# Gate and up blocks by Strassen's seven products for three of eight k-tile pairs, and the feed forward in parts of 4, 4 and 3 blocks

## The chip, the cores and the metric

The kernel runs on one core of one Trainium2 chip. The core has a matrix engine (PE, which reads its stationary operand through a weight load, PEld), a vector engine (DVE), a scalar engine (ACT), GpSimd (POOL) and a queue engine (SP) that issues DMAs. The metric is the device time of one execution in microseconds (us).

## What is computed

The input is 256 tokens of width 2048 in float32. The reference runs two blocks: a hybrid layer (an mLSTM and a gated delta net side by side), and a layer of dilated attention and gated linear attention followed by a feed forward. The change is in that feed forward, which is the last stage:

```
h = rmsnorm(x, ffn_norm_w[l])
x = x + (jax.nn.silu(h @ w_gate[l]) * (h @ w_up[l])) @ w_down[l]
```

`w_gate` and `w_up` are 2048 x 5632, `w_down` is 5632 x 2048, all float32. A final rmsnorm follows.

## The kernel before

**Every product is three matmuls.** A float32 matrix is split into a high part (`fp32r`, the rounded value) and a low part (the difference). A product is `hi x wh + hi x wl + lo x wh`. The activations' `hi` and `lo` (tiles `hl`, `pg`) are stationary operands of 128 x 128; the weights' `wh` and `wl` are the moving operands, 512 columns wide, and the sums stand in PSUM (tile `mm`), one bank for each half `t` of the 256 tokens.

**The weight stream.** All weights of the whole kernel pass through one list of pieces in a fixed order. A piece is up to three k-tiles (128 rows) of a 512-column block, at most 1536 columns wide (`WN`). For piece `i` the stream issues the load of piece `i + 3` on SP (tile `wr`, `RB` = 3 buffers), then the split of pieces up to `i + 2`, then the matmuls of piece `i`. The split (`cut`, L259 and L260) is a cast on ACT into `wh`, and then a subtraction on DVE into `wl`; `wh` and `wl` have three buffers each. So ACT can cast a piece only when PE has finished with the piece that held the buffer, three pieces earlier. What follows a finished chunk (its activation function, transposes, the operand for the next stage) runs as a generator in `sides`, one step for each piece or so.

**The feed forward.** It runs in two halves of 2816 hidden columns, each of five blocks of 512 columns and one of 256. For each block a gate chunk (16 k-tiles, two banks) is followed by `ff_gate` (tanh on ACT, two DVE operations), then an up chunk, then `ff_up`: multiply, transpose by PE (L203), cast on ACT (L1354) and subtraction on DVE (L1355) into the operand for the down projection. After each half come four down chunks of 22 k-tiles, each ended by `ff_down`, two DVE operations that add into the residual `hw`.

**The order of instructions.** A scheduler orders each engine's queue when the program is built; each engine then works its queue in order. [...]

Of the kernel before, what the change touches and what calls it, by code (L numbers as in the profile page):

```python
# [11 lines left out]
F32 = mybir.dt.float32  # L12
# [25 lines left out]
HALF = HID // 2  # L38


C_ID, C_TRIU, C_TRIL, C_MNEG, C_SEG, C_ONE, C_HB, C_VEC = 0, 128, 256, 384, 512, 768, 770, 818
# [56 lines left out]
        self.po = None  # L98


class Opnd:


    def __init__(self, n):
        self.t = [None] * n
        self.cols = [0] * n

    def ready(self, k):
        return self.cols[k] == 1
# [7 lines left out]

    def lo(self, k, t=None):
        return self.part(1, k, t)

@with_exitstack
def kernel(ctx, tc, a, out, dbg=None):
# [35 lines left out]
    def v3(t, b):  # L160
        return t.rearrange("p (a b) -> p a b", b=b)
# [72 lines left out]

# [2 lines left out]
    def load(i):  # L237
        if i >= len(pieces) or i in raw:
            return
        ch, k, n = pieces[i]  # L240
        w = wp.tile([P, WN], F32, tag="wr", name=nm("wr"), bufs=RB)
        wv = v3(w[:, :n * ch.width], ch.width)
        c = 0
        for src in ch.src:
            cw_ = src.shape[1]
            SP.dma_start(out=wv[:, :, c:c + cw_],  # L246
                         in_=src[(ch.k0 + k) * P:(ch.k0 + k + n) * P, :].rearrange("(k p) n -> p k n", p=P))
            c += cw_
# [29 lines left out]
    def products(ch, k0, tiles, ks, o):  # L278

        for j in ks:  # L280
# [10 lines left out]
            else:  # L291
# [3 lines left out]
                mm(po, wl, hi, start=False, stop=False)  # L295
                mm(po, wh, lo, start=False, stop=last)

    def run_stream():
        i = 0
        while i < len(pieces):  # L300
            ch, k0, _ = pieces[i]

            many = LAST if i == len(pieces) - LAST else 1
            for j in range(many):
                load(i + j + 3)
            for j in range(3):
                cut(i + j)
            tiles = []
# [62 lines left out]
    def vec(row):  # L371
        return vt[:, row:row + 1]
# [926 lines left out]
    sc3 = cst.tile([P, 2], F32, name="sc3")  # L1299
    st_3 = {"n": 0}  # L1300

    def mix_out(po, n):
        h = v3(hw[n], 512)
        for t in range(2):
# [9 lines left out]
        yield from operand(h, op3, 4 * n, 4, lambda j: vec(V_FN + 4 * n + j), act3["t"][0], act3["t"][1], 4 * n)  # L1314
        if n == 3:
            m_ = small(2, "ms2")
            V.tensor_reduce(out=m_, in_=v3(ss3, 4), axis=AX.X, op=ALU.add)
# [2 lines left out]
            ts(r3h, r3, 0.5)  # L1320
            stt(sc3, r3, 0.5, r3, ALU.mult, ALU.mult)

    opf = [Opnd(44), Opnd(44)]
    gate = {}

    def ff_gate(po, key, w):

        n = page()[:, :2 * w]
        n3 = v3(n, w)
        for t in range(2):  # L1330
            act(n3[:, t, :], po[t][:, :w], AF.Tanh, scale=r3h[:, t:t + 1])
# [32 lines left out]
    def ff_down(po, n, hf):  # L1364
# [4 lines left out]
        if hf == 1:  # L1369
# [111 lines left out]
    for hf in range(2):  # L1481
        off = 0
        while off < HALF:
            w = min(512, HALF - off)
            c0 = hf * HALF + off
            add(Chunk([wg[:, c0:c0 + w]], w, 16, op3, lambda po, c0=c0, w=w: ff_gate(po, c0, w)))
            add(Chunk([wu[:, c0:c0 + w]], w, 16, op3, lambda po, c0=c0, hf=hf, w=w: ff_up(po, c0, w, hf, c0 // P)))
            off += w
        for n in range(4):
            add(Chunk([wd[:, n * 512:(n + 1) * 512]], 512, HALF // P, opf[hf],  # L1490
                      lambda po, n=n, hf=hf: ff_down(po, n, hf), k0=hf * HALF // P))
# [25 lines left out]
```

## Time and profile before

| what | value |
|---|---|
| three runs | 2348.87, 2351.42, 2351.17 us; median 2351.17 |
| the profiled execution | 2350.77 us, of which the span from the first to the last instruction is 2349.0 us |
| busy share of the span | PE 99%, weight load 82%, DVE 59%, ACT 45%, POOL 4% |
| granted PE clock, mean | 0.998 of full speed |
| gate and up loads begin | 1600.0 us |
| last output DMA issued from | 2341.2 us |

Busy time is the time in which an engine had an instruction in work. A chain of waits names what the end of the program waited for, step by step backwards.

### The profile page before, as it was taken

The numbers are of one execution on the slowest core, as the hardware profiler recorded it, in microseconds if no ns is written. First come the engines' busy times: TensorE is split into PE (matmuls) and PEld (weight loads), VectorE is DVE, ScalarE is ACT, GpSimd is POOL, SyncE is SP. The second block draws the span as 40 slices with busy tenths as digits, with TensorE's granted clock in tenths as the row PEclk, the third lists the DMA queues.
The fourth block names the chain that finished last, engine by engine and source line by source line (L and its number), as shares of the span: only waits on it lengthen the run. The fifth ranks groups of instructions, "written<-read, shape, count | busy, mean of one in ns | idle before, by whom it ended". The sixth has DMA issues, their size and how long they took to land.

```text
span 2349.0 us, 28535 instructions
## 1 busy us (share of the span) xinstructions
PE 2330.5 (99%) x11392; PEld 1930.0 (82%) x11392; DVE 1384.8 (59%) x1689; ACT 1062.6 (45%) x1240; POOL 91.1 (4%) x122
## 2 busy tenths in 40 slices
PE   8999999999999999999999999999999999999998
PEld 6888888888888888888887877888888888888886
DVE  6778677686576555455555566655545544555554
ACT  5554444544454444444444465444444333434443
POOL 0101001000000000000000000000000000000000
PEclk9999999999999999999999999999999999999999
DMA  6656545665555556566565544556655555665554
GB/s 207 188 177 202 180 142 157 188 196 188 169 159 163 180 188 210 184 200 210 180 219 179 157 141 130 166 180 201 188 192 186 191 191 187 192 194 187 188 197 152
DMA packets 226340, 427.89 MB, mean 182 GB/s; under 512 B 17256, under 2 KB 25872, under 8 KB 226208
## 3 DMA queue, kind: packets, MB, share of 16 engines
q1 hardware_dynamic: 220288, 411.07, 54.7%
q0 software_dynamic: 5056, 13.70, 2.1%
q8 instruction: 89, 1.46, 0.2%
q10 hardware_dynamic: 864, 1.31, 0.2%
q14 instruction: 43, 0.35, 0.0%
HBM read 422.31 MB, written 3.73 MB: 181 GB/s over the span
## 4 chain that ended last, share of the span: by engine, by line
PE 98%; DMA 1%; ACT 0%; issue 0%; DVE 0%; SPq 0%; POOLq 0%; POOL 0%; ACTq 0%; DVEq 0%
PE mm L185 91%; PE sp L185 4%; PE sp L203 3%; PE sp L699 1%; PE sp L1129 0%; DMA wr<-in_w_in_dram 0%; DMA pg<-in_x_dram 0%; ACT pg L182 0%; DVE wl L260 0%; ACT wh L259 0%; ACT hl L182 0%; SPq L246 0%; DVE pg L179 0%; ACT hp L182 0%; POOLq L1513 0%
## 5 line engine op out<-in xcount | busy, mean ns | idle before, releaser
L185 PE MATMUL mm<-wh,hl 128*128 128x512 f32 (+1 forms) x4864 | 1500.1, 387 | 1.6 <-ACT wh L259 1.6
L260 DVE TENSOR_TENSOR wl<-wr,wh 128x1536 fp32r<-128x1536 f32 (+3 forms) x588 | 919.3, 1567 | 751.6 <-ACT wh L259 750.7
L259 ACT CAST wh<-wr 128x1536 fp32r<-128x1536 f32 (+3 forms) x588 | 780.4, 1328 | 994.7 <-PE mm L185 943.1
L185 PEld LDWEIGHTS mm<-wh,hl 128*128 128x128 f32 x4864 | 904.7, 188 | 183.2 <-issue 4.9
L185 PE MATMUL mm<-wl,hl 128*128 128x512 f32 (+1 forms) x2432 | 941.9, 387 | 1.3 <-DVE wl L260 1.3
L185 PEld LDWEIGHTS mm<-wl,hl 128*128 128x128 f32 x2432 | 458.0, 188 | 89.7 <-DVE wl L260 1.9
L185 PE MATMUL mm<-wh,pg 128*128 128x512 f32 x1472 | 456.0, 390 | 0.0
L185 PEld LDWEIGHTS mm<-wh,pg 128*128 128x128 f32 x1472 | 276.2, 188 | 57.0
L185 PE MATMUL mm<-wl,pg 128*128 128x512 f32 x736 | 287.4, 390 | 0.0
L185 PEld LDWEIGHTS mm<-wl,pg 128*128 128x128 f32 x736 | 138.2, 188 | 29.2 <-DVE wl L260 0.9
L203 PE MATMUL sp<-con,pg 128*128 128x128 f32 x555 | 88.3, 275 | 4.1 <-DMA pg<-in_consts_dram 4.0
L203 PEld LDWEIGHTS sp<-con,pg 128*128 128x128 f32 x555 | 68.9, 141 | 21.0 <-issue 6.0
L179 DVE SCALAR_TENSOR_TENSOR pg<-cv,vt,pg 128x255 f32<-128x255 f32 (+2 forms) x144 | 61.4, 478 | 7.6 <-ACT pg L182 7.5
L185 PE MATMUL sp<-pg,pg 128*128 128x128 f32 (+3 forms) x320 | 50.7, 316 | 0.0
L179 DVE SCALAR_TENSOR_TENSOR pg<-pg,mm 128x512 f32<-128x512 f32 (+1 forms) x60 | 39.9, 665 | 16.5 <-ACT pg L182 14.8
L185 PEld LDWEIGHTS sp<-pg,pg 128*128 128x128 f32 (+1 forms) x320 | 43.0, 190 | 6.1 <-issue 2.5
L182 ACT ACTIVATE pg<-mm,rh 128x512 f32<-128x512 f32 x40 | 27.2, 687 | 33.8 <-PE mm L185 33.8
L182 ACT ACTIVATE pg<-pg 128x512 f32<-128x512 f32 (+2 forms) x54 | 35.3, 676 | 12.1 <-DVE pg L792 4.9
L182 ACT ACTIVATE pg<-mm,rstd 128x512 f32<-128x512 f32 x36 | 24.4, 687 | 32.2 <-PE mm L185 32.2
L182 ACT ACTIVATE pg<-sp,vt 128x256 fp32r<-128x256 f32 (+1 forms) x48 | 21.5, 471 | 25.7 <-PE sp L203 14.4
L179 DVE SCALAR_TENSOR_TENSOR hl<-sp,vt,hl 128x256 fp32r<-128x256 f32 x48 | 21.7, 479 | 14.0 <-ACT hl L182 13.9
L182 ACT ACTIVATE hl<-sp,vt 128x256 fp32r<-128x256 f32 x48 | 21.2, 478 | 16.1 <-PE sp L203 10.9
(245 smaller groups left out, 871.2 us busy)
## 6 DMA issues: line engine op xcount, KB each, us to landing
wr<-in_w_in_dram SPq DMA_DIRECT2D x208, 768.0 KB, 4.5
wr<-in_w_in_dram SPq DMA_DIRECT2D x104, 512.0 KB, 4.6
wr<-in_w_out_dram SPq DMA_DIRECT2D x48, 768.0 KB, 4.5
wr<-in_w_down_dram SPq DMA_DIRECT2D x48, 768.0 KB, 4.4
wr<-in_w_gate_dram SPq DMA_DIRECT2D x42, 768.0 KB, 4.4
wr<-in_w_up_dram SPq DMA_DIRECT2D x42, 768.0 KB, 4.4
wr<-in_w_out_dram SPq DMA_DIRECT2D x24, 512.0 KB, 5.1
wr<-in_w_gate_dram SPq DMA_DIRECT2D x20, 512.0 KB, 4.8
```

The lines of the kernel that those rows point to most:

```text
L179: return V.scalar_tensor_tensor(out=o, in0=x, scalar=s, in1=y, op0=op0, op1=op1)
L182: return A.activation(out=o, in_=x, func=f, **kw)
L185: PE.matmul(o, l, r, start=start, stop=stop)
L203: PE.transpose(o, x, ident[:n, :n])
L259: A.copy(out=h[:, :sz], in_=w[:, :sz])
L260: V.tensor_tensor(out=l[:, :sz], in0=w[:, :sz], in1=h[:, :sz].bitcast(F32), op=ALU.subtract)
L699: PE.matmul(o, l, r_, start=True, stop=True, tile_position=(row, col))
```

## The change

**Seven products.** A pair of k-tiles, two halves of the tokens, and gate and up side by side make a 2 x 2 by 2 x 2 product of blocks of 128 x 128 by 128 x 512. Before, that is eight products (24 matmuls). For pairs 1, 3 and 5 of the eight pairs of a block (`SPAIRS`, counted there from 0) the new kernel forms Strassen's seven products (Winograd's form, 21 matmuls) in three pieces: A (three products: 9 matmuls, 1536 columns to split), B and C (two products: 6 matmuls and 1024 columns each). The extra operands are sums: of the activations, made once in `operand3`; of the weights, made on DVE for each piece A by three subtractions (`cut`). Of C nothing is loaded; it is a page that these subtractions fill. The other five pairs stay at eight products in two pieces, X (the gate's two k-tiles) and Y (the up's), 12 matmuls and 1024 columns each. Seven sums stand in seven banks; `ff_mid` and `ff_done` add them up on DVE.

**Parts.** There are eleven blocks of 512, in parts of 4, 4 and 3 (`PARTS`), each part followed by its four down chunks (16, 16 and 12 k-tiles). The raw buffers `wr` become four, and the scratch of the POOL-issued DMAs goes from 8192 to 2048 bytes.

```diff
-RB = 3
+RB = 4
+AHEAD = 3
+SPAIRS = (0, 2, 4)
+PARTS = ((0, 4), (4, 8), (8, 11))
...
+    PLAN = {"X": (("2", "a0"), ("4", "a1")), "Y": (("5", "a1"), ("3", "d")),
+            "A": (("1", "a0", 0), ("2", "a0", 1), ("3", "s4", 2)),
+            "B": (("5", "s1", 0), ("7", "s3", 1)),
+            "C": (("6", "s2", 0), ("4", "a1", 1))}
...
+        elif part in "XY":
+            get(w[:, :1024], ch.src[part], k, 2)
+        elif part == "A":
+            get(w[:, :1024], ch.src["X"], k, 2)
+            get(w[:, 1024:], ch.src["Y"], k + 1, 1)
+        elif part == "B":
+            get(w[:, :512], ch.src["Y"], k, 1)
...
+        if part == "A":
+
+            w2, w3 = raw[i + 1], page()
+            raw[i + 2] = w3
+            V.tensor_tensor(out=v3(w2[:, 512:], 512), in0=mid(w2[:, :512], 2), in1=v3(w, 512)[:, 0::2, :], op=ALU.subtract)
+            V.tensor_tensor(out=w3[:, :512], in0=w[:, 1024:], in1=w2[:, 512:1024], op=ALU.subtract)
+            V.tensor_tensor(out=w3[:, 512:1024], in0=w[:, 512:1024], in1=w3[:, :512], op=ALU.subtract)
+        x = w[:, 512:] if part == "B" else w[:, :{None: n * ch.width, "X": 1024, "Y": 1024, "A": 1536, "C": 1024}[part]]
...
+    def pair_products(ch, e, k0, part, wh, wl):
...
+            for q in js:
...
+                mm(po, hi, wh[:, q, :], start=first, stop=False)
+                mm(po, hi, wl[:, q, :], start=False, stop=False)
+                mm(po, lo, wh[:, q, :], start=False, stop=last)
...
+            ch.po = {b: pm.tile([P, 512], F32, tag="mm", name=nm("mm")) for b in "2453"}
+        if part == "A" and "1" not in ch.po:
+            for b in "176":
+                ch.po[b] = ps.tile([P, 512], F32, tag="sp", name=nm("mm"))
...
+    def ff_mid(po, st):
+
+        x, v = page(), page()
+        A.copy(out=x[:, :512], in_=po["1"])
+        V.tensor_tensor(out=x[:, 512:], in0=x[:, :512], in1=po["6"], op=ALU.add)
+        V.tensor_tensor(out=v[:, :512], in0=x[:, 512:], in1=po["7"], op=ALU.add)
...
+    def ff_done(po, st, part, k0):
...
+        V.tensor_tensor(out=g[:, lo_], in0=x[:, lo_], in1=po["2"], op=ALU.add)
+        V.tensor_tensor(out=g[:, hi_], in0=v[:, lo_], in1=po["4"], op=ALU.add)
+        V.tensor_tensor(out=v[:, hi_], in0=x[:, hi_], in1=po["5"], op=ALU.add)
+        V.tensor_tensor(out=v[:, lo_], in0=v[:, lo_], in1=po["5"], op=ALU.add)
+        V.tensor_tensor(out=v[:, hi_], in0=v[:, hi_], in1=po["3"], op=ALU.add)
+        for t, c in ((0, lo_), (1, hi_)):
+            act(x[:, c], g[:, c], AF.Tanh, scale=r3h[:, t:t + 1])
+        yield
+        stt(g, x, 1.0, g, ALU.add, ALU.mult)
+        mul(g[:, lo_], g[:, lo_], v[:, hi_])
+        mul(g[:, hi_], g[:, hi_], v[:, lo_])
...
-        while off < HALF:
-            w = min(512, HALF - off)
...
+    for part, (b0, b1) in enumerate(PARTS):
+        for blk in range(b0, b1):
...
-    nc = bacc.Bacc("TRN2", target_bir_lowering=False, num_devices=1, dynamic_dma_scratch_size=8192)
+    nc = bacc.Bacc("TRN2", target_bir_lowering=False, num_devices=1, dynamic_dma_scratch_size=2048)
```

In the queues below, line numbers of the new kernel differ: L217 is the matmul (before L185), L317 the cast and L319 the subtraction of a split (before L259, L260), L311 to L313 the three subtractions for a piece A, L1484 to L1488 the five sums of `ff_done`, L211 and L202 a helper for its products.

DVE's queue before, where an up chunk ends and the next gate chunk follows. `wl` is a split's output, L170 multiplies by the up sums, L1355 makes the down operand:

```order
L260 TENSOR_TENSOR wl2031_12757<-wr2026_12730,wh2030_12756 128x1536
L170 TENSOR_TENSOR pg2011_12639<-pg2011_12639,mm2015_12650 128x512
L170 TENSOR_TENSOR pg2011_12639<-pg2011_12639,mm2016_12651 128x512
L260 TENSOR_TENSOR wl2034_12783<-wr2029_12754,wh2033_12782 128x1536
L260 TENSOR_TENSOR wl2042_12810<-wr2032_12780,wh2041_12809 128x1024
L1355 TENSOR_TENSOR pg2038_12801<-sp2039_12802,pg2037_12800 128x512
L260 TENSOR_TENSOR wl2045_12836<-wr2040_12807,wh2044_12835 128x1536
```

The same queue of the new kernel between the second and the third block. The rows begin behind the split of the last piece Y (`wl2094`) and L312; `wl2098`, `wl2100`, `wl2104` and `wl2114` are the next block's A, B, C and first X:

```order
L313 TENSOR_TENSOR pg2096_12895<-wr2092_12874,pg2096_12895 128x512
L1484 TENSOR_TENSOR pg2101_12931<-pg2081_12815,mm2034_12600 128x512
L319 TENSOR_TENSOR wl2098_12901<-wr2092_12874,wh2097_12899 128x1536
L1485 TENSOR_TENSOR pg2101_12931<-pg2082_12816,mm2035_12601 128x512
L319 TENSOR_TENSOR wl2100_12917<-wr2095_12893,wh2099_12915 128x1024
L1486 TENSOR_TENSOR pg2082_12816<-pg2081_12815,mm2036_12602 128x512
L1487 TENSOR_TENSOR pg2082_12816<-pg2082_12816,mm2036_12602 128x512
L1488 TENSOR_TENSOR pg2082_12816<-pg2082_12816,mm2037_12603 128x512
L319 TENSOR_TENSOR wl2104_12943<-pg2096_12895,wh2103_12941 128x1024
L211 SCALAR_TENSOR_TENSOR pg2101_12931<-pg2081_12815,pg2101_12931 128x1024
L311 TENSOR_TENSOR wr2121_12998<-wr2121_12998,wr2118_12983 128x1024
L319 TENSOR_TENSOR wl2114_12968<-wr2102_12939,wh2113_12966 128x1024
```

Between two splits there stood at most two rows of 512 columns before; now the sums of the finished block, the subtractions for two pieces A and a product of 1024 columns stand between them.

PE's queue of the new kernel at the same place: the last matmuls of B, those of C and X that need `wh` alone, and the first that needs X's `wl2114`:

```order
L217 MATMUL mm2107_12947<-wl2100_12917,pg1888_11793 128x512
L217 MATMUL mm2107_12947<-wh2099_12915,pg1888_11793 128x512
L217 MATMUL mm2106_12946<-wh2103_12941,hl1878_11738 128x512
L217 MATMUL mm2105_12945<-wh2113_12966,hl1878_11738 128x512
L217 MATMUL mm2106_12946<-wl2104_12943,hl1878_11738 128x512
L217 MATMUL mm2106_12946<-wh2103_12941,hl1878_11738 128x512
L217 MATMUL mm2106_12946<-wh2113_12966,hl1878_11738 128x512
L217 MATMUL mm2107_12947<-wh2119_12986,hl1878_11738 128x512
L217 MATMUL mm2108_12948<-wh2119_12986,cv1897_11858 128x512
L217 MATMUL mm2105_12945<-wl2114_12968,hl1878_11738 128x512
```

The scheduler has brought seven matmuls of C, X and Y forward, ahead of the first that reads `wl2114`; before, a piece's matmuls stood in their own order with whole pieces of 12 or 18.

ACT's queue of the new kernel a little later, around the block's second triple (pair 3): the casts of Y, A, B, C and of the X and Y behind them; L1506 belongs to the finished block:

```order
L317 CAST wh2119_12986<-wr2112_12964 128x1024
L317 CAST wh2123_13004<-wr2118_12983 128x1536
L317 CAST wh2126_13025<-wr2121_12998 128x1024
L1506 CAST pg2115_12976<-sp2117_12978 128x512
L317 CAST wh2129_13045<-pg2122_13000 128x1024
L317 CAST wh2132_13060<-wr2128_13043 128x1024
L317 CAST wh2135_13073<-wr2131_13058 128x1024
```

The cast of C (`wh2129`) reads a page that DVE writes (L312, L313), so it waits for DVE, and the casts of X and Y stand behind it; before, every cast read a loaded tile.

## Rows read from the trace of the kernel before

**Rows 1.** The page: the span, the busy time of each engine, and the granted PE clock in 40 slices.

```profile
span 2349.0 us, 28535 instructions
PE 2330.5 (99%) x11392; PEld 1930.0 (82%) x11392; DVE 1384.8 (59%) x1689; ACT 1062.6 (45%) x1240; POOL 91.1 (4%) x122
PEclk9999999999999999999999999999999999999999
```

**Rows 2.** The page: the chain of waits that ended last, by engine.

```profile
PE 98%; DMA 1%; ACT 0%; issue 0%; DVE 0%; SPq 0%; POOLq 0%; POOL 0%; ACTq 0%; DVEq 0%
```

**Rows 3.** The chain of waits in order of time, inside the feed forward: start us, length us, what, how many. L185 is the matmul, L203 a transpose; the last row is of the block of 256 columns.

```profile
1661.83 39.27 PE mm L185 x173
...
1705.89 0.44 PE sp L203 x4
1706.32 5.72 PE mm L185 x25
...
1833.61 2.27 PE mm L185 x19
```

**Rows 4.** Busy time in three stretches: from the first gate load issued of one block of 512 columns to that of the next, the block of 256 columns, and a half's down chunks. Columns: length, then busy us and instructions of PE, PEld, DVE, ACT, POOL, then granted PE clock, DMA share, GB/s.

```profile
1635.39:1679.89 44.50, 44.50 (x202) 36.77 (x201) 22.79 (x18) 18.52 (x16) 0.00 (x0) 1.00 0.61 189
1813.39:1836.95 23.56, 23.56 (x134) 20.71 (x133) 11.73 (x9) 9.31 (x8) 0.00 (x0) 1.00 0.64 209
1836.95:1958.44 121.49, 121.49 (x606) 103.46 (x605) 58.76 (x44) 45.20 (x35) 0.00 (x0) 1.00 0.56 191
```

**Rows 5.** Groups of instructions by shape: line, engine, operation, out<-in, shape, count, busy us, mean ns of one, idle time before and what ended it. The first eight are from 1600 us on, the last three of the whole trace.

```profile
L260 DVE TENSOR_TENSOR wl<-wr,wh 128x1536 fp32r<-128x1536 f32 x132 | 232.0, 1758 | 272.1 <-ACT wh L259 272.1
L259 ACT CAST wh<-wr 128x1536 fp32r<-128x1536 f32 x132 | 195.5, 1481 | 282.4 <-PE mm L185 282.4
L260 DVE TENSOR_TENSOR wl<-wr,wh 128x1024 fp32r<-128x1024 f32 x56 | 68.6, 1225 | 45.3 <-ACT wh L259 45.3
L259 ACT CAST wh<-wr 128x1024 fp32r<-128x1024 f32 x56 | 59.0, 1054 | 81.6 <-PE mm L185 81.6
L1355 DVE TENSOR_TENSOR pg<-sp,pg 128x512 fp32r<-128x512 f32 x22 | 15.1, 688 | 10.1 <-ACT pg L1354 10.0
L182 ACT ACTIVATE pg<-mm,r3h 128x512 f32<-128x512 f32 x20 | 13.8, 691 | 19.0 <-PE mm L185 19.0
L170 DVE TENSOR_TENSOR pg<-pg,mm 128x512 f32<-128x512 f32 x20 | 13.7, 684 | 3.1 <-PE mm L185 3.1
L179 DVE SCALAR_TENSOR_TENSOR pg<-mm,sc,pg 128x512 f32<-128x512 f32 x16 | 12.0, 748 | 8.1 <-PE mm L185 7.1
...
L179 DVE SCALAR_TENSOR_TENSOR pg<-pg,pg 128x1024 f32<-128x1024 f32 x10 | 12.2, 1220 | 0.7 <-ACT pg L182 0.6
L170 DVE TENSOR_TENSOR pg<-pg,pg 128x1024 f32<-128x1024 f32 x4 | 4.9, 1224 | 0.1
L775 DVE TENSOR_TENSOR pg<-pg,hp 128x512 f32<-128x512 f32 x4 | 2.7, 684 | 0.0
```

**Rows 6.** The timeline of DVE and ACT: start us, length us, engine, line, what, idle time before and what ended it. First ACT in an earlier stage, then both engines in the feed forward.

```profile
942.65 0.69 ACT L182 ACTIVATE pg<-mm,rh 128x512 f32<-128x512 f32 x1 [1.12 <-PE mm L185]
943.23 1.47 ACT L259 CAST wh<-wr 128x1536 fp32r<-128x1536 f32 x1
...
1694.03 1.76 DVE L260 TENSOR_TENSOR wl<-wr,wh 128x1536 fp32r<-128x1536 f32 x1 [3.28 <-ACT wh L259]
1695.70 0.68 DVE L170 TENSOR_TENSOR pg<-pg,mm 128x512 f32<-128x512 f32 x1
...
1699.31 1.06 ACT L259 CAST wh<-wr 128x1024 fp32r<-128x1024 f32 x1 [1.24 <-PE mm L185]
1700.40 1.23 DVE L260 TENSOR_TENSOR wl<-wr,wh 128x1024 fp32r<-128x1024 f32 x1 [0.53 <-ACT wh L259]
```

**Rows 7.** Who waited for whom from 1600 us on: total us, times, longest us.

```profile
ACT wh L259 <- PE mm L185: 374.5, 178, 3.0
DVE wl L260 <- ACT wh L259: 328.6, 183, 3.3
```

**Rows 8.** DMA issues: count, KB each, median us from issue to landing. The first two are from 1640 to 1812 us (gate and up), the third from 1840 to 1950 us (down).

```profile
wr<-in_w_gate_dram SPq DMA_DIRECT2D x16, 768.0 KB, 4.4
...
wr<-in_w_gate_dram SPq DMA_DIRECT2D x7, 512.0 KB, 5.3
...
wr<-in_w_down_dram SPq DMA_DIRECT2D x7, 512.0 KB, 3.7
```

**Rows 9.** Stretches with waits of PE, as in rows 4: two of the start, and the end.

```profile
8.00:12.00 4.00, 2.89 (x19) 2.34 (x17) 1.36 (x3) 3.72 (x12) 0.00 (x0) 1.00 0.96 295
...
24.00:28.00 4.00, 2.58 (x11) 1.47 (x9) 1.50 (x1) 3.00 (x6) 0.00 (x0) 1.00 0.70 258
...
2311.00:2349.00 38.00, 28.74 (x127) 23.47 (x125) 15.39 (x17) 12.57 (x18) 1.12 (x2) 0.93 0.35 126
```

**Rows 10.** Who waited in the whole trace: PE for split weights, and two of the waits for DMAs that POOL issues; the engine that waits comes first.

```profile
PE mm L185 <- ACT wh L259: 1.6, 2, 0.9
PE mm L185 <- DVE wl L260: 1.5, 3, 1.1
...
POOL hp L690 <- DMA xo<-pg: 6.1, 2, 3.1
POOL pg L583 <- DMA li<-pg: 5.3, 2, 3.4
```

More of the change, by code (lines that the diff above doesn't have):

```diff
@@ L98, in __init__ @@
         self.po = None
+class Pair:
+    kind, width = "pair", 512
+    PLAN = {"X": (("2", "a0"), ("4", "a1")), "Y": (("5", "a1"), ("3", "d")),
+            "A": (("1", "a0", 0), ("2", "a0", 1), ("3", "s4", 2)),
+            "B": (("5", "s1", 0), ("7", "s3", 1)),
+            "C": (("6", "s2", 0), ("4", "a1", 1))}
+    def __init__(self, x, y, nk, opnd, pairs, mid, done):
+        self.src, self.nk, self.opnd, self.mid, self.done, self.k0 = {"X": x, "Y": y}, nk, opnd, mid, done, 0
+        self.parts = []
+        for p in range(nk // 2):
+            self.parts += [(2 * p, 2, c) for c in ("ABC" if p in pairs else "XY")]
+        self.last_s = max(i for i, q in enumerate(self.parts) if q[2] == "C")
+        self.po = None
+        use = [(i, t[0]) for i, q in enumerate(self.parts) for t in self.PLAN[q[2]]]
+        self.first = {b: min(i for i, c in use if c == b) for _, b in use}
+        self.final = {b: max(i for i, c in use if c == b) for _, b in use}
 class Opnd:
@@ L224, in add @@
         chunks.append(ch)
+        if ch.kind == "pair":
+            pieces.extend((ch, k, n, c) for k, n, c in ch.parts)
+            return ci
         m = -(-ch.nk // ch.per)
@@ L239, in load, with get @@
             return
-        ch, k, n = pieces[i]
+        ch, k, n, part = pieces[i]
+        if part == "C":
+            raw[i] = None
+            return
         w = wp.tile([P, WN], F32, tag="wr", name=nm("wr"), bufs=RB)
[L242 to L248, printed above, removed]
-        raw[i] = w
+        raw[i] = w
+        def get(o, src, k, n):
+            SP.dma_start(out=v3(o, src.shape[1]) if n > 1 else o,
+                         in_=src[k * P:(k + n) * P, :].rearrange("(k p) n -> p k n", p=P) if n > 1 else src[k * P:(k + 1) * P, :])
+        if part is None:
+            wv = v3(w[:, :n * ch.width], ch.width)
+            c = 0
+            for src in ch.src:
+                cw_ = src.shape[1]
+                SP.dma_start(out=wv[:, :, c:c + cw_],
+                             in_=src[(ch.k0 + k) * P:(ch.k0 + k + n) * P, :].rearrange("(k p) n -> p k n", p=P))
+                c += cw_
+        elif part in "XY":
[5 more added lines that the diff above has]
+            get(w[:, :512], ch.src["Y"], k, 1)
     def cut(i):
@@ L296, in products, with run_pair @@
                 mm(po, wh, lo, start=False, stop=last)
+    def pair_products(ch, e, k0, part, wh, wl):
+        plan = ch.PLAN[part]
+        for n, (bk, f, *j) in enumerate(plan):
+            js = j or (0, 1)
+            for q in js:
+                po = ch.po[bk]
+                hi, lo = ch.opnd.form(f, k0, q if f in ("a0", "a1", "d") else 0) if part in "XY" else ch.opnd.form(
+                    f, k0, 0 if bk == "1" else 1 if f[0] == "a" else 0)
+                first = ch.first[bk] == e and q == js[0]
+                last = ch.final[bk] == e and q == js[-1]
+                mm(po, hi, wh[:, q, :], start=first, stop=False)
+                mm(po, hi, wl[:, q, :], start=False, stop=False)
+                mm(po, lo, wh[:, q, :], start=False, stop=last)
+            if n == len(plan) - 1:
+                advance()
+    def run_pair(ch, i, e):
+        _, k0, n, part = pieces[i]
+        wh, wl = split.pop(i)
+        while not all(ch.opnd.ready(k0 + j) for j in range(n)):
+            assert sides, "operand never ready"
+            advance()
+        if ch.po is None:
+            ch.po = {b: pm.tile([P, 512], F32, tag="mm", name=nm("mm")) for b in "2453"}
+        if part == "A" and "1" not in ch.po:
+            for b in "176":
+                ch.po[b] = ps.tile([P, 512], F32, tag="sp", name=nm("mm"))
+        pair_products(ch, e, k0, part, wh, wl)
+        g = ch.mid(ch.po) if e == ch.last_s else ch.done(ch.po) if e == len(ch.parts) - 1 else None
+        if g is not None:
+            next(g)
+            sides.append(g)
     def run_stream():
@@ L300, in run_stream @@
         while i < len(pieces):
-            ch, k0, _ = pieces[i]
+            ch, k0, _, part = pieces[i]
             many = LAST if i == len(pieces) - LAST else 1
             for j in range(many):
-                load(i + j + 3)
+                load(i + j + AHEAD)
             for j in range(3):
                 cut(i + j)
+            if part is not None:
+                e = 0 if pieces[i - 1][0] is not ch else e + 1
+                run_pair(ch, i, e)
+                i += 1
+                continue
             tiles = []
@@ L1480 @@
         add(Chunk([wo2[:, n * 512:(n + 1) * 512]], 512, 16, opm, lambda po, n=n: mix_out(po, n)))
[L1481 to L1488 removed]
+    for part, (b0, b1) in enumerate(PARTS):
+        for blk in range(b0, b1):
+            st = {}
+            c = slice(blk * 512, (blk + 1) * 512)
+            add(Pair(wg[:, c], wu[:, c], 16, op3, SPAIRS, lambda po, st=st: ff_mid(po, st),
+                     lambda po, st=st, part=part, blk=blk: ff_done(po, st, part, 4 * blk)))
         for n in range(4):
[L1490 to L1491 removed]
+            add(Chunk([wd[:, n * 512:(n + 1) * 512]], 512, 4 * (b1 - b0), opf[part],
+                      lambda po, n=n, part=part: ff_down(po, n, part), k0=4 * b0))
     startup()
```

94 lines of the change are left out of this document (65 added, 29 removed).

## The prediction

> **What bounds the kernel now.** I read the busy times first: PE is busy 2330.5 of 2349.0 us at a granted clock that shows 9 in every slice [rows 1]. The chain of waits says the same: 98% of it is PE [rows 2]. So only fewer PE instructions, or new waits of PE, can move the end by much. The third view is the stretch that changes. From one block to the next PE is busy all 44.50 us while DVE is busy 22.79 and ACT 18.52 [rows 4]: half of DVE is free. The fourth view says why DVE is idle. ACT waits 374.5 us for PE before its casts, and DVE 328.6 us for ACT before its subtractions [rows 7]: with three buffers, the split of a piece begins only when PE is done with an earlier piece. DVE's free time is spread between the pieces, and DVE cannot run ahead by more than that. This decides whether new DVE work is hidden.
>
> **What the change removes.** PE passes a matmul of 512 columns each 39.27/173 = 0.227 us, and a transpose each 0.44/4 = 0.11 us [rows 3]. A block is 192 matmuls and 8 transposes: 192 x 0.227 + 0.88 = 44.46 us, as measured [rows 4]. Three pairs lose 3 matmuls each, so a block loses 9, and eleven blocks 99: 99 x 0.227 = 22.5 us. The two blocks of 256 columns go too. One takes 23.56 us where half a large block is 22.25 [rows 4]; twice 1.31 is 2.6 us. Both together: 25.1 us. A new block is 183 x 0.227 + 0.88 = 42.4 us of PE.
>
> The down projection keeps its matmuls. It has four more endings of chunks, each two DVE operations of 748 ns [rows 5], 6.0 us in all; a half's down chunks leave DVE idle for 121.49 - 58.76 us [rows 4], so this costs nothing. Without that cover it would be 6.0 us.
>
> **What the change adds on DVE.** Per block, with durations of the same shapes [rows 5]: splits 3 x 1.758 + 16 x 1.225 = 24.9; the subtractions for three pieces A 3 x (1.22 + 2 x 0.684) = 7.8; two sums in `ff_mid` and five in `ff_done` 7 x 0.684 = 4.8; the multiplications 1.22 + 2 x 0.684 = 2.6; the down operand 2 x 0.688 = 1.4. That is 41.4 us in 40 instructions, instead of 22.79. Instructions that follow each other directly overlap: a subtraction begun at 1694.03 runs 1.76 us, and the next starts at 1695.70, 0.09 us before its end [rows 6]. With some 32 of the 40 back to back this is 2.9 us less: DVE has 38.5 to 41.4 us of work in 42.4 us of PE. On average it fits. But a triple A, B, C gives PE 21 x 0.227 = 4.8 us and asks 1.758 + 2 x 1.225 + 2.59 = 6.8 us of DVE, so it falls behind at each triple and must have a lead to lose.
>
> [...]
>
> **Where PE will wait.** I follow the queues by hand, with 0.05 us for a hand-over between engines (a cast that ends at 1700.37 lets DVE start at 1700.40 [rows 6], 0.03) and 0.09 us of overlap.
>
> *Block boundary.* Let PE end X of pair 7 at t = 0; this frees the buffers for the last Y. Its cast (1.054 us) ends at 1.1 and its split at 2.4, with the subtraction L311 done beside the cast. If L311 starts only then, because its load is late, the split ends at 3.3. Behind it stand 13 rows of DVE up to the split of the next block's first X: L312, L313, five sums, four splits, L211 and L311, in all 7 x 0.684 + 1.758 + 3 x 1.225 + 2 x 1.22 = 12.7 us. Less ten overlaps and plus three hand-overs this is 11.9, so X's `wl` is ready at 14.3 to 15.2. PE has 36 matmuls of Y, X and Y left, 9 of A, 6 of B and 7 that were brought forward: 58 x 0.227 = 13.2 us. PE waits 1.1 to 2.0 us; I take 1.7, as loads of 512 KB are the slow ones (below). The first matmul of Y that was brought forward waits for its own cast, some 0.2 us.
>
> *Second triple.* Matmuls of the first C were put behind Y, so the cast of A takes the buffer that X leaves; t = 0 where PE ends that X. Cast 0.05 to 1.53, split of A to 3.3, split of B, L1507 and L312 to 5.7, then L313 and the cast of C that reads its result, with a hand-over each: ready at 7.5 to 7.7. PE has 28 matmuls and 8 transposes, 7.24 us: a wait of 0.3 to 0.5. Then X's cast, which stands behind C's on ACT, comes 0.95 us later where PE has two matmuls, 0.45 us: 0.5 more. Together 0.9.
>
> *Third triple.* A's buffer is free early here, so C comes at most 0.1 late; the cast of X behind it costs the same 0.5: 0.6.
>
> That is 1.7 + 0.2 + 0.9 + 0.6 = 3.4 us for each of the eight boundaries between blocks inside a part (2.4 to 3.8 by the bounds): 27 us. The first blocks of the three parts have no `ff_done` ahead, and I give them only the casts behind C, 1.0 us each: 3. Loads: pieces of 1024 columns are loads of 512 KB, and these took 5.3 us to land among gate and up pieces against 4.4 for 768 KB [rows 8]. The fourth raw buffer lets them start earlier; from below they cost nothing more, from above 0.9 us at three places of eight boundaries, 22 us. As loads are issued three pieces ahead, some 7 us, I take a tenth of that, 2.5. PE's waits: 27 + 3 + 2.5 = 32.5 us.
>
> **What else changes.** Ahead of the feed forward PE waits 1.6 + 1.5 us for split weights [rows 10]; a fourth raw buffer may give back some of it: -1 (0 to -3). The scratch of POOL's DMAs is smaller. In the rows POOL itself waits for such DMAs, longest 3.4 us [rows 10]; no row prices a small scratch. As no such wait of PE stands out, I take 0, and from above one such wait, 3.4 us.
>
> **The sum.** The profiled execution took 2350.8 us (span 2349.0 and 1.8 around it), 0.4 below the median. 2350.8 - 25.1 - 1 + 32.5 = **2357 us**, slightly slower. This kernel can tell 0.2% (4.7 us) from no change.
>
> **Rivals.**
> *The waits stay hidden (faster).* DVE's work fits the time on average, and each wait above is a small difference of two large sums. If the boundary wait is nil, because the first L311 always finds its data and the overlap is a little larger, and the triples keep their lower bounds of 0.8 and 0.5, then 8 x 1.3 + 3 = 13 us of waits and 2350.8 - 25.1 - 1 + 13 = 2338 us; if these vanish too, 2325. Against it: three stalls would have to close, and the price of each sits in rows of measured durations. It decides at (25.1 + 1 - 3)/8 = 2.9 us per boundary: less is faster than before.
> *Loads land late.* Of the 19 pieces of a block ten are loads of 512 KB, the slow kind [rows 8], and they follow each other. If the 0.9 us falls on two or three of three places, waits grow by 14 to 22 us: 2371 to 2379. Against it: the DMA share is 0.61 [rows 4], and the bytes per us hardly rise.
> *No overlap on DVE.* The 0.09 us are read where no sum is in the way. Without them the boundary grows by 10 x 0.09 and each of the other places by 0.27: 1.4 x 8 = 12 us, 2369.
> *PE's clock falls in the new gaps.* [...] Against it: with PE busy only 2.58 and 2.89 of 4.00 us at the start, the granted clock stands at 1.00, and only the idle end shows 0.93 [rows 9]. [...]
>
> **How the numbers follow.** The forecast with waits of 22 to 40 us (2347 to 2364) has 0.55: 0.25 of it within 0.2% (2346.5 to 2355.9), 0.30 above. Hidden waits 0.17, late loads 0.20, no overlap 0.04, clock 0.03, something else, such as POOL's scratch, 0.01. So faster 0.17, same 0.25, slower 0.58. The range leaves out the lower rival and the top of the late loads: 2343 to 2380. The forecast's own range is 2347 to 2364.
>
> **What would show it.** Right: 99 fewer matmuls; the clock at 1.00 inside the blocks; DVE busy above 80% from one gate load to the next and that period about 46 us, not 42.4; PE's waits in the feed forward 20 to 45 us, three places a block, most of them for `wl` at the first X of a block and for `wh` of C and the X behind it; down chunks without waits. Wrong: a period of 43 us (hidden), waits of casts or of L311 for loads (late loads), a start-to-start distance of DVE rows equal to their length (no overlap), or a clock below 1.00 behind the gaps.

## The result and the profile after

| | before | after |
|---|---|---|
| median | 2350.65 us (2348.87 to 2351.42) | 2370.39 us (2367.51 to 2373.01) |
| profiled execution: span | 2349.0 us | 2368.0 us |
| PE busy | 2330.5 us | 2326.6 us |

The ratio is 1.0085 (95% interval 1.0067 to 1.0102): 0.85% slower, 20 us, where 2357 us was forecast.

The page after: span, busy time and the chain by engine, to be read against [rows 1, 2]:

```profile
span 2368.0 us, 28594 instructions
...
PE 2326.6 (98%) x11101; PEld 1903.1 (80%) x11101; DVE 1572.4 (66%) x1952; ACT 1127.1 (48%) x1342; POOL 91.3 (4%) x122
...
PE 91%; DVE 4%; DMA 2%; ACT 1%; issue 1%; SPq 0%; DVEq 0%; POOLq 0%; POOL 0%; ACTq 0%
```

PE has 291 fewer instructions: 192 went with the blocks of 256 columns (the run without triples below has 11200), 99 with the triples. And 9% of the chain now belongs to others: PE waits. The busy time hides how much, because the record of a matmul (0.39 us) is longer than the distance to the next one (0.227), so 0.16 us of each wait is under the record of the matmul ahead. The weight loads (0.19 us) don't cover a wait in this way. So the second view is who waited for whom in the feed forward, with the rows of PEld:

```profile
ACT wh L317 <- PE mm L217: 320.8, 179, 7.2
DVE wl L319 <- ACT wh L317: 164.4, 112, 4.0
...
PEld mm L217 <- DVE wl L319: 24.5, 15, 2.4
DVE wr L311 <- DMA wr<-in_w_up_dram: 23.2, 17, 3.7
...
PEld mm L217 <- ACT wh L317: 21.1, 45, 0.7
...
PE mm L217 <- DVE wl L319: 18.2, 11, 2.0
...
PE mm L217 <- ACT wh L317: 6.6, 24, 0.4
```

PEld waits 24.5 + 21.1 us in 60 places; PE's own rows show only 24.8 of it. The kernel before had no such row in its feed forward. Against the sum 2350.8 - 25.1 - 1.8 (start) = 2323.9 us the median is 46.5 us late: these waits are about of that size. The agreement is partly chance: a weight load's row can show more than PE loses (1.78 us ahead of the wait at 1706.44, where the matmul comes 1.51 us late), and the falls of the clock below are lost time that no row of waits has. By the distances between the starts of PE's instructions the feed forward loses 45.7 us, some 4.5 of them to the clock. New is also that DVE waits 23.2 us for loads, at L311.

The third view: two stretches from one block's first wait for X to the next one's, the second and the first period of part 1, as in [rows 4]:

```profile
1706.44:1752.87 46.43, 44.21 (x191) 34.65 (x191) 38.80 (x41) 23.67 (x24) 0.00 (x0) 1.00 0.57 181
1658.49:1706.44 47.95, 45.78 (x191) 35.81 (x192) 38.89 (x41) 23.65 (x24) 0.00 (x0) 0.96 0.55 176
```

A period takes 46.43 us for 42.4 us of PE work, with DVE busy 38.80 us (84%) and the clock at 1.00. The first period is 1.52 us longer, at a granted clock of 0.96.

The fourth view: PE's waits in the steady period, in order of time (start, length, what, and in brackets the wait ahead):

```profile
1706.44 0.50 PE L217 MATMUL mm<-wl,hl 128*128 128x512 f32 x1 [1.35 <-DVE wl L319]
...
1716.72 0.50 PE L217 MATMUL mm<-wh,pg 128*128 128x512 f32 x1 [0.38 <-ACT wh L317]
...
1717.67 0.49 PE L217 MATMUL mm<-wh,hl 128*128 128x512 f32 x1 [0.23 <-ACT wh L317]
...
1728.56 0.50 PE L217 MATMUL mm<-wh,hl 128*128 128x512 f32 x1 [0.22 <-ACT wh L317]
```

These are the three places of the prediction: `wl` of the block's first X, the casts of C and of X in the second triple, and the cast of X in the third. And DVE's queue ahead of the first of them:

```profile
1700.57 0.68 DVE L1487 TENSOR_TENSOR pg<-pg,mm 128x512 f32<-128x512 f32 x1
1701.17 0.68 DVE L1488 TENSOR_TENSOR pg<-pg,mm 128x512 f32<-128x512 f32 x1
1701.77 1.22 DVE L319 TENSOR_TENSOR wl<-pg,wh 128x1024 fp32r<-128x1024 f32 x1
1702.90 1.22 DVE L211 SCALAR_TENSOR_TENSOR pg<-pg,pg 128x1024 f32<-128x1024 f32 x1
1704.04 1.22 DVE L311 TENSOR_TENSOR wr<-wr,wr 128x1024 f32<-128x1024 f32 x1
1705.17 2.35 DVE L319 TENSOR_TENSOR wl<-wr,wh 128x1024 fp32r<-128x1024 f32 x2
```

DVE never rests here: sums, products and a subtraction for the next triple stand ahead of the split (1705.17) that PE waits for.

The fifth view is the chain at the first boundary of part 1, which shows a second cause: start, length, what.

```profile
1639.29 5.01 DMA wr<-in_w_up_dram
...
1644.42 0.06 DVE wr L311
1644.48 1.08 issue
1645.56 1.22 DVE wl L319
...
1656.09 1.22 DVE wr L311
1657.30 1.15 DVE wl L319
...
1658.49 3.84 PE mm L217 x9
```

L311 starts when the load of a piece B lands, and the split of the last Y, whose cast was ready before, stands behind it on DVE. The 12 us of queue that follow are as in the other blocks, but begin later, and PE waits 1.98 us instead of 1.35. Behind this wait the clock fell; stretches of 4 us from there, and from a wait of 2.02 us in the first block of part 2:

```profile
1652.00:1656.00 4.00, 3.53 (x14) 2.13 (x13) 4.00 (x6) 2.71 (x3) 0.00 (x0) 1.00 0.72 255
1656.00:1660.00 4.00, 2.02 (x8) 1.25 (x7) 4.00 (x5) 0.00 (x0) 0.00 (x0) 0.87 0.13 15
1660.00:1664.00 4.00, 4.00 (x14) 3.24 (x13) 0.78 (x2) 1.32 (x1) 0.00 (x0) 0.70 0.70 249
1664.00:1668.00 4.00, 4.00 (x22) 3.22 (x21) 3.70 (x4) 1.79 (x3) 0.00 (x0) 1.00 0.00 1
1892.00:1896.00 4.00, 4.00 (x19) 3.31 (x18) 1.23 (x1) 2.85 (x4) 0.00 (x0) 1.00 0.58 206
1896.00:1900.00 4.00, 1.98 (x9) 1.33 (x8) 4.00 (x4) 1.00 (x1) 0.00 (x0) 1.00 0.15 19
```

At 1656 and 1660 the granted clock is 0.87 and 0.70, and PE passes 14 matmuls in 4 us instead of 17 or 18: for some 3 us matmuls start 0.43 us apart instead of 0.227. This happened behind the first boundary of each part, three times: waits of 1.98, 1.96 and 1.98 us, and then a granted clock of 0.70, 0.57 and 0.64 in the lowest 4 us. The same idle time at 1896, with no shorter wait close ahead of it, left the clock at 1.00. But in the run without the last sums (below) a wait of 2.04 us that ended at 1887.34, also with none close ahead, was followed by a fall:

```profile
1884.00:1888.00 4.00, 1.96 (x9) 1.33 (x8) 3.07 (x4) 1.61 (x2) 0.00 (x0) 1.00 0.01 3
1888.00:1892.00 4.00, 4.00 (x12) 3.15 (x11) 3.29 (x3) 0.68 (x1) 0.00 (x0) 0.57 0.75 226
```

So shorter waits ahead are not needed for a fall, and what decides between these cases stays open.

### The profile page after: what moved, and what is told of

It reads as the page before. It is cut to its first block, busy times and chain, and to the rows that moved or that the text cites. A ratio compares the mean times of both kernels' runs of the same rounds, so it can differ in the third digit from the quotient of the medians.

```text
span 2368.0 us, 28594 instructions
## 1 busy us (share of the span) xinstructions
PE 2326.6 (98%) x11101; PEld 1903.1 (80%) x11101; DVE 1572.4 (66%) x1952; ACT 1127.1 (48%) x1342; POOL 91.3 (4%) x122
## 4 chain that ended last, share of the span: by engine, by line
PE 91%; DVE 4%; DMA 2%; ACT 1%; issue 1%; SPq 0%; DVEq 0%; POOLq 0%; POOL 0%; ACTq 0%
PE mm L217 83%; PE sp L217 4%; DVE wl L319 3%; PE sp L235 2%; DMA wr<-in_w_up_dram 1%; ACT wh L317 1%; PE sp L798 1%; PE sp L1228 0%; DVE wr L311 0%; DMA pg<-in_x_dram 0%; DVE pg L211 0%; DVE pg L1484 0%; DMA wr<-in_w_in_dram 0%; DVE pg L1485 0%; DVE pg L1488 0%
## 5 line engine op out<-in xcount | busy, mean ns | idle before, releaser
L217 PE MATMUL mm<-wh,hl 128*128 128x512 f32 x4186 | 1342.5, 395 | 3.6 <-ACT wh L317 3.6
L319 DVE TENSOR_TENSOR wl<-wr,wh 128x1536 fp32r<-128x1536 f32 (+2 forms) x632 | 940.5, 1494 | 548.0 <-ACT wh L317 545.9
L317 ACT CAST wh<-wr 128x1536 fp32r<-128x1536 f32 (+2 forms) x632 | 800.6, 1270 | 925.6 <-PE mm L217 862.8
L217 PEld LDWEIGHTS mm<-wh,hl 128*128 128x128 f32 x4186 | 786.6, 188 | 177.8 <-ACT wh L317 14.3
L217 PE MATMUL mm<-wl,hl 128*128 128x512 f32 x2093 | 826.0, 395 | 18.9 <-DVE wl L319 18.6
L217 PE MATMUL mm<-wh,pg 128*128 128x512 f32 x1780 | 563.9, 391 | 3.4 <-ACT wh L317 3.0
L217 PEld LDWEIGHTS mm<-wl,hl 128*128 128x128 f32 x2093 | 395.1, 189 | 105.4 <-DVE wl L319 25.6
L217 PEld LDWEIGHTS mm<-wh,pg 128*128 128x128 f32 x1780 | 334.0, 188 | 76.0 <-ACT wh L317 6.8
L217 PE MATMUL mm<-wl,pg 128*128 128x512 f32 x890 | 348.6, 392 | 0.0
L217 PEld LDWEIGHTS mm<-wl,pg 128*128 128x128 f32 x890 | 167.1, 188 | 36.5 <-DVE wl L319 0.9
L235 PEld LDWEIGHTS sp<-con,pg 128*128 128x128 f32 x555 | 70.4, 144 | 21.1 <-issue 6.3
L211 DVE SCALAR_TENSOR_TENSOR pg<-cv,vt,pg 128x255 f32<-128x255 f32 (+2 forms) x144 | 61.2, 476 | 6.5 <-ACT pg L214 6.3
L217 PE MATMUL mm<-wh,cv 128*128 128x512 f32 x176 | 61.4, 390 | 0.0
L319 DVE TENSOR_TENSOR wl<-pg,wh 128x1024 fp32r<-128x1024 f32 x33 | 40.3, 1222 | 27.9 <-ACT wh L317 27.8
L311 DVE TENSOR_TENSOR wr<-wr,wr 128x1024 f32<-128x1024 f32 x33 | 40.4, 1223 | 24.3 <-DMA wr<-in_w_up_dram 23.9
L317 ACT CAST wh<-pg 128x1024 fp32r<-128x1024 f32 x33 | 34.7, 1051 | 44.9 <-PE mm L217 24.6
L217 PE MATMUL sp<-pg,pg 128*128 128x128 f32 (+3 forms) x320 | 50.7, 316 | 0.0
L217 PEld LDWEIGHTS sp<-pg,pg 128*128 128x128 f32 (+1 forms) x320 | 43.0, 190 | 6.1 <-issue 2.5
```

What stands on the lines that cost most here:

```text
L211: return V.scalar_tensor_tensor(out=o, in0=x, scalar=s, in1=y, op0=op0, op1=op1)
L217: PE.matmul(o, l, r, start=start, stop=stop)
L235: PE.transpose(o, x, ident[:n, :n])
L311: V.tensor_tensor(out=v3(w2[:, 512:], 512), in0=mid(w2[:, :512], 2), in1=v3(w, 512)[:, 0::2, :], op=ALU.subtract)
L317: A.copy(out=h[:, :sz], in_=x)
L319: V.tensor_tensor(out=l[:, :sz], in0=x, in1=h[:, :sz].bitcast(F32), op=ALU.subtract)
```

## The experiments

The theory: DVE's work is too late at the boundaries and triples, since the sums of the finished block and the subtractions of the weights stand ahead of splits in its queue. The first rival: the loads come late, whatever DVE has to do. Times are medians beside those of the kernel before in the same comparison (2350.2 to 2351.4 us).

**No triples.**

```diff
-SPAIRS = (0, 2, 4)
+SPAIRS = ()
...
+        A.copy(out=v[:, lo_], in_=po["5"])
+        V.tensor_tensor(out=v[:, hi_], in0=v[:, lo_], in1=po["3"], op=ALU.add)
```

With no triple the end of a block needs the four banks of X and Y alone; the last two lines are of that.

> No pair goes by seven products; the eleven blocks, the pieces X and Y of two k-tiles, the parts, the fourth raw buffer and the small scratch stay. Theory (the new work on DVE makes PE wait, the rest of the change costs nothing): PE has all 99 matmuls again, no waits of PE in the feed forward and no fall of the clock there; 2351.2 - 2.6 (blocks of 256 columns gone) - 1.8 (start) = 2347 us, 2343 to 2351. Rival (the smaller pieces and the 512 KB loads come late whatever DVE does): PE still waits 10 to 25 us in the feed forward and the time is 2357 to 2372.

2345.5 us, ratio 0.9979 (0.9971 to 0.9988), and a stretch as in [rows 4] in which PE never rests:

```profile
1640.00:1684.50 44.50, 44.50 (x201) 36.72 (x201) 23.77 (x24) 19.48 (x21) 0.00 (x0) 1.00 0.60 190
```

So the smaller pieces, the parts, the fourth buffer and the small scratch together cost nothing: 2350.6 - 2.6 - 1.8 would be 2346.2. The triples bring all of the loss.

**No subtractions of the weights.**

```diff
-            V.tensor_tensor(out=v3(w2[:, 512:], 512), in0=mid(w2[:, :512], 2), in1=v3(w, 512)[:, 0::2, :], op=ALU.subtract)
-            V.tensor_tensor(out=w3[:, :512], in0=w[:, 1024:], in1=w2[:, 512:1024], op=ALU.subtract)
-            V.tensor_tensor(out=w3[:, 512:1024], in0=w[:, 512:1024], in1=w3[:, :512], op=ALU.subtract)
+        if part is not None and part in "BC":
+            x = mid(w[:, :512], 2)
```

> The three subtractions of the weights for each piece A are left out; B and C split the loaded 512 columns of Y twice instead, so the products are not those of the reference, but every split, matmul, sum and load stands as in the change. Theory (DVE is late by these 2.6 us per triple and the cast of C waits for them): the boundary wait of 2.4 us and the 0.5 + 0.4 us of C and X in the later triples go, the falls of the clock go with them; of 46 us at most 10 stay and the time is 2328 to 2338. Rival (loads land late): the casts of A and B wait for the loads instead of L311, PE keeps half of its waits or more, 2347 to 2370.

2331.4 us, ratio 0.9920 (0.9906 to 0.9933), inside the theory's range. PEld's waits fall to a fifth:

```profile
PEld mm L217 <- DVE wl L319: 5.2, 8, 0.7
PEld mm L217 <- ACT wh L317: 4.9, 16, 0.4
```

This can't tell the two causes apart completely, since without L311 no DVE instruction waits for B's load either.

**No last sums.**

```diff
-        V.tensor_tensor(out=v[:, hi_], in0=x[:, hi_], in1=po["5"], op=ALU.add)
-        V.tensor_tensor(out=v[:, lo_], in0=v[:, lo_], in1=po["5"], op=ALU.add)
-        V.tensor_tensor(out=v[:, hi_], in0=v[:, hi_], in1=po["3"], op=ALU.add)
```

> The last three sums of a finished block (L1486 to L1488) are left out and the multiplication takes another page, so the result isn't the reference's; all else stands as in the change. Theory (the sums between the splits make the boundary wait): 1.8 us less DVE work at eight boundaries takes the wait of 1.5 + 0.7 us to about 0.4, the falls of the clock behind the first boundaries go: 2347 to 2358. Rival (at the boundary PE waits for something else, a load or a buffer): 2364 to 2371.

2343.7 us, ratio 0.9975 (0.9965 to 0.9985): 27 us better than the change and 3 us below the range. But the gain isn't where the theory had it. The waits for `wl` did not shrink (24.9 us here, 24.5 in the change). What is gone from the list are PE's waits for casts, 21.1 us at the weight loads, and the falls of the clock behind the first boundaries (one came in a first block instead, shown above; the mean granted clock is 0.997 instead of 0.995):

```profile
PEld mm L217 <- DVE wl L319: 24.9, 23, 2.5
```

I read this so: a boundary that ends late passes its lateness to the triples behind it, and 1.8 us less of DVE work per block is enough to stop that.

**The triples later.**

```diff
-SPAIRS = (0, 2, 4)
+SPAIRS = (2, 4, 6)
```

> The triples stand at pairs 3, 5 and 7 instead of 1, 3 and 5: the same work, but the sums of the finished block no longer share DVE with a triple. Theory (the sums of the block and a triple's work meet at the boundary): the boundary wait of 2.4 to 3.4 us at eight boundaries goes and with it the falls of PE's clock (5 us); 1.0 to 2.5 us per block stay at the triples, 11 to 28 us; 2336 to 2353. Rival (every triple costs the same wherever it stands, as DVE needs 6.8 us where PE has 4.8): no gain beyond 4 us, 2366 to 2374.

2334.1 us, ratio 0.9924 (0.9912 to 0.9937): the same work, 36 us faster than the change, and 2 us better than the theory's range: the triples of the inner blocks cost nothing to be seen once DVE isn't behind when they begin. What is left are three waits of PE, one in the first block of each part, and one fall of the clock, to 0.59 over 4 us, behind the longest of them, 3.25 us. DVE's timeline at the first:

```profile
1629.03 1.23 DVE L319 TENSOR_TENSOR wl<-pg,wh 128x1024 fp32r<-128x1024 f32 x1 [1.50 <-ACT wh L317]
1632.69 1.22 DVE L311 TENSOR_TENSOR wr<-wr,wr 128x1024 f32<-128x1024 f32 x1 [2.44 <-DMA wr<-in_w_up_dram]
1633.84 1.22 DVE L319 TENSOR_TENSOR wl<-wr,wh 128x1024 fp32r<-128x1024 f32 x1
```

DVE stands idle for 2.44 us in front of L311 until B's load is there; the split at 1633.84 has to wait behind it, and PE waits 2.03 us for that split.

**The subtractions on POOL.**

```diff
-            V.tensor_tensor(out=v3(w2[:, 512:], 512), in0=mid(w2[:, :512], 2), in1=v3(w, 512)[:, 0::2, :], op=ALU.subtract)
+            G.tensor_tensor(out=v3(w2[:, 512:], 512), in0=mid(w2[:, :512], 2), in1=v3(w, 512)[:, 0::2, :], op=ALU.subtract)
```

and likewise the other two.

> The three subtractions of the weights run on POOL, which is idle in the feed forward, instead of DVE. If POOL needs no more than twice DVE's 2.6 us for a triple and doesn't slow DVE, DVE's chains shorten by 2.6 us at each triple and the time is 2330 to 2350. If POOL needs three times as long or more, B and C come later than now, each triple costs 2 us more than now, and the time is above 2390. If POOL and DVE slow each other, DVE's subtractions of 1024 columns show more than 1.23 us.

2385.5 us, ratio 1.0149 (1.0135 to 1.0163): slower than the change, between the cases; the last sentence came true. POOL's and DVE's timelines at one triple:

```profile
1692.85 2.40 POOL L311 TENSOR_TENSOR wr<-wr,wr 128x1024 f32<-128x1024 f32 x1 [13.86 <-DMA wr<-in_w_up_dram]
1695.33 2.16 POOL L312 TENSOR_TENSOR pg<-wr,wr 128x512 f32<-128x512 f32 x1
1697.57 2.69 POOL L313 TENSOR_TENSOR pg<-wr,pg 128x512 f32<-128x512 f32 x1
```

```profile
1691.23 1.22 DVE L319 TENSOR_TENSOR wl<-wr,wh 128x1024 fp32r<-128x1024 f32 x1 [1.73 <-ACT wh L317]
1693.50 2.83 DVE L319 TENSOR_TENSOR wl<-wr,wh 128x1024 fp32r<-128x1024 f32 x1 [1.04 <-ACT wh L317]
...
1699.03 0.68 DVE L1485 TENSOR_TENSOR pg<-pg,mm 128x512 f32<-128x512 f32 x1
```

The split of 1.22 us takes 2.83 while POOL works; the sum L1485, one of whose inputs is in PSUM, keeps its 0.68 us beside L313. POOL needs 7.2 us for a triple's 2.6 us of DVE, and slows DVE as well.

**B's load first.**

```diff
+        if part == "A":
+            load(i + 1)
         w = wp.tile([P, WN], F32, tag="wr", name=nm("wr"), bufs=RB)
```

> The load of a piece B (256 KB) is issued ahead of the two loads of its piece A instead of behind them, so that L311, which needs B and the gate's part of A, no longer waits for the last of three loads. The scheduler then also puts the split of the next block's first X ahead of L311 in DVE's queue. Theory (late loads hold up DVE's queue through L311, and this makes the long waits behind which PE's clock falls): 8 boundaries give back 1.1 us by the order, the first boundary of each part 0.5 to 1 us more, the falls of the clock (5 us) go, the first blocks of the parts give 1.2 us each: 2350 to 2357. Rival (the loads do not matter, DVE's own work does): only the order's part, 2358 to 2363. Second rival (A's part of Y is now last and its cast waits): 2366 to 2375.

2355.7 us, ratio 1.0024 (1.0014 to 1.0034): 15 us better than the change, as the theory of late loads had it in sum, though not in its parts. Three waits in the first blocks are gone (1.55, 2.02 and 1.93 us by PE's rows), the first boundary now waits like the others, and no fall of the clock is left behind it (mean granted clock 0.999 instead of 0.995). But the inner periods did not get shorter:

```profile
1653.52:1699.79 46.27, 44.58 (x191) 34.60 (x191) 38.71 (x41) 23.68 (x24) 0.00 (x0) 1.00 0.56 182
1699.79:1746.62 46.83, 44.98 (x192) 34.62 (x192) 38.80 (x41) 23.70 (x24) 0.00 (x0) 1.00 0.56 180
```

The wait for X's `wl` fell from 1.35 to 0.61 us, since the scheduler put this split ahead of a subtraction, and the same time came back as waits for sums in the banks (L1489 and L1490, which are L1487 and L1488 of the change; 7 us) and for casts. In the inner periods the new order gave nothing; what came back lies in the first blocks, at the first boundaries and in the clock, where the change's loads were late.

**Three raw buffers.**

```diff
-RB = 4
+RB = 3
```

> Three raw buffers as before instead of four, all else as in the change. Theory (the fourth buffer gives 1.8 us at the start, and L311 already waits for loads with four): the 1.8 us at the start are lost and the feed forward loses 3 to 12 us more at L311 and the casts: 2374 to 2385. Rival (loads are issued by the buffers' release anyway): only the start is lost, 2371 to 2373.

2395.8 us, ratio 1.0193 (1.0179 to 1.0207): 25 us slower than the change, beyond the theory's range in its direction. Not only L311 waits for loads now (40.1 instead of 23.2 us), ACT's casts do too:

```profile
ACT wh L317 <- DMA wr<-in_w_up_dram: 53.1, 41, 4.4
PEld mm L217 <- ACT wh L317: 49.5, 73, 2.0
DVE wr L311 <- DMA wr<-in_w_up_dram: 40.1, 31, 2.9
```

**Later triples and B's load first.** Both edits.

> The triples at pairs 3, 5 and 7, and the load of B ahead of those of A. Theory: what is left with the late triples, three waits of 2.0 to 3.2 us of PE behind an L311 that waits for B's load, and the fall of the clock behind the longest, shrinks by 5 to 8 us: 2326 to 2330. Rival (the wait goes over to A's own loads): 2332 to 2336.

2328.3 us, ratio 0.9907 (0.9894 to 0.9921): the fastest of all, faster than the kernel before by 0.9%, and 4.4 us above the 2323.9 us without any wait. The stretch from one block's transposes to the next one's:

```profile
1704.91:1747.63 42.72, 42.72 (x194) 35.01 (x192) 38.57 (x41) 23.76 (x24) 0.00 (x0) 1.00 0.61 197
```

DVE has the same work as in the change (38.57 against 38.80 us), now in 42.7 us: it was never too much. Its place, and loads that came late, made the waits.

**One pair earlier.** `SPAIRS = (1, 3, 5)`, and B's load first.

> The triples at pairs 2, 4 and 6, and the load of B ahead of A's: one plain pair stands between the boundary and the first triple, and two behind the last. Theory (one plain pair has room for the sums, as its two splits take 2.5 us of DVE while PE has 24 matmuls, 5.4 us): as good as pairs 3, 5 and 7, 2326 to 2332. Rival (the finished block's sums and products, 6 us of DVE, need more than that room): part of the boundary wait is back, 1 us at each of eight boundaries, 2334 to 2342.

2369.0 us, ratio 1.0079 (1.0065 to 1.0092): as slow as the change, and 13 us slower than B's load first alone. The rival had the mechanism, and its price was far too low. Sums, products and the down operand of a finished block are 7.4 us of DVE; one plain pair gives 5.4 - 2.5 = 3 us of room, two pairs 6. With one pair DVE enters the first triple late, and a plain pair between triples (3 us of room) hardly pays for a triple (2 us too much). By this the lateness stays for the whole block, and a period is indeed as long as in the change:

```profile
1657.25:1704.13 46.88, 44.24 (x192) 34.35 (x192) 38.98 (x41) 23.63 (x24) 0.00 (x0) 1.00 0.56 180
```

The sum of room doesn't say why pairs 2, 4 and 6 do worse than pairs 1, 3 and 5 with the same order of loads. The first subtraction of a triple also waits more for loads here (30.3 us in 29 places, against 18.5 in 16), so late loads have a part that no run separates.

**Four triples.** `SPAIRS = (1, 3, 5, 6)`, and B's load first.

> Four triples in a block (pairs 2, 4, 6 and 7) and the load of B ahead of A's. PE has 33 matmuls less than with three triples (7.5 us). Theory (DVE's whole work per block is the next limit): DVE needs 38.1 us in a block with late triples and 4.1 us more with a fourth, 42.2 us, where PE would have 41.7; DVE becomes the bound inside the parts and every hand-over adds to it: 2332 to 2350, slower than three triples. Rival (only the place of the work counts, DVE catches up in the down chunks): 2319 to 2326.

2376.7 us, ratio 1.0108 (1.0094 to 1.0122): slower, as the theory of DVE's whole work had it, by more than its range. The first triple stands behind one plain pair here too, which by the run before costs 40 us by itself; so this run doesn't show what a fourth triple alone costs.

## Why the prediction was right, and where it was off

The measured time lies in the stated range, 2343 to 2380, but above the forecast's own, 2347 to 2364. It is about where the rival of late loads put it, 2371 to 2379 with a chance of 0.20. That rival had the size and not the places: it put 0.9 us at places of all eight inner boundaries, and the runs show the loss in the first blocks, at the first boundaries and in the clock. So the nearness of its number is partly luck. Two of the signs of being wrong appeared as well: L311 waited for loads, and the clock fell below 1.00.

**The saving** was as worked out. The best version comes within 4.4 us of the sum without waits, so 25.1 us are there to be had.

**DVE's work and its overlap** were right: 38.80 us per period against 38.5 to 41.4, and the subtractions still start 0.09 us before the end of the one ahead. The rival without overlap did not happen.

**PE's waits at the inner boundaries** were at the right places and near in size: 46.43 - 42.4 = 4.0 us each, 32 in all, against 3.4 and 27. The boundary wait for `wl` was 1.35 us in the row and 1.5 with what the matmul's record covers, against 1.7; the matmuls of Y that were brought forward lost 0.2 us, as forecast (two distances took 0.67 us, from 1704.03 to 1704.70, where twice 0.227 is 0.45); and after the waits the second matmul starts 0.33 to 0.34 instead of 0.227 us behind the first (0.37 and 0.44 at 1931.74 and 2204.88, where the clock fell), which the sum did not have.

**The late loads are the step that failed.** I took a tenth of 22 us (the sum has 2.5 where that is 2.2), because loads are issued some 7 us ahead. With B's load first 15 us come back. By the starts of PE's instructions 13.5 of them lie in the feed forward: 3 x 2 us in the first blocks, 3 x 1 at the first boundaries (X's wait went from 1.98 to 0.61 us, and part of that came back as other waits), and three falls of the clock at 1.5 us. The 7 us were not there. A's two loads were issued at 1637.31 and 1637.73, but B's only at 1639.29, when the split begun at 1638.04 had ended; it took 5.01 us to land, and DVE had been free for L311 since 1641.97. I had asked what a late load costs the split that needs it, and not what stands behind L311 on DVE: a split of another piece, already cast. My 3 us for the first blocks were half of what was lost there, and were meant for casts, for which PE did not wait there.

**The clock** was a rival with a chance of 0.03. It fell at three of the eight boundaries, for 1.5 us each, behind waits of 2 us with shorter ones close ahead. But waits of 2.02 us at 1896 and of 2.04 us in the run without the last sums, both alone, ended in different clocks, 1.00 and 0.57, so no run here shows what makes it fall.

**The start** gave 1.84 us (the last operations ahead of the feed forward, at 1584.01 us on DVE before, start at 1582.17), against 1. The first gate load was issued at 1589.93 us before (1600.0, as the table of the time before has it, is the third) and at 1586.36 us now. The scratch was not tried by itself. Without triples the sum closes within 1 us, which leaves little room for a cost of it.

2350.8 - 25.1 - 1.8 + 32 + 13.5 = 2369.4 us is the sum as the runs have it; the profiled execution took 2369.8, and the median is 2370.4. The direction rested on the inner boundaries, and they were right. (The stated range was said to leave out the top of the late loads; with 2380 above their 2379 it didn't.)

## What to carry to other kernels

When work moves to an engine that is half idle, compare its work with the time piece by piece, from the point where it last had a lead: with B's load first, the same 39 us of work per block left PE 45 us behind the sum without waits or 4, by whether one or two plain pairs stood between the block's end and the first triple. In a queue that is worked in order, as DVE's was here (with the triples later it stood idle for 2.44 us ahead of L311, and PE waited 2.03 us for the split behind it), ask of each instruction that waits for a load what stands behind it, and issue first the load that the earliest of them needs. Don't add up PE's waits from the idle time ahead of matmuls, as their records cover 0.16 us of each; take the distances between starts.

## What was not expected of the hardware

Beside POOL's subtraction a DVE split of two SBUF inputs took 2.83 instead of 1.22 us, and a product of two pages 1.63 instead of 0.68 on average, while sums with one input in PSUM kept 0.68 us. A granted clock of 0.70 over 4 us is visible in short stretches only; the page's 40 slices show 9 throughout. Two waits of PE of nearly the same length, 2.02 and 2.04 us, with none close ahead, left the clock at 1.00 in one run and were followed by 0.57 in the other.
